# An encoder trunk in fp32r with its normed inputs and weights at their own offsets in longer buffers

## The chip, the cores and the metric

The kernel runs on one core of one Trainium2 chip. The metric is the time on the device in microseconds (us) from the start to the end of one execution, as the median of several. The core has five engines with a queue of instructions each: TensorE (PE in the profile, with its weight loads shown apart as PEld), VectorE (DVE), ScalarE (ACT), GpSimd (POOL) and SyncE (SP), which in this kernel issues most DMA transfers. All work on one on-chip memory of 128 partitions.

## What is computed

A trunk of two layers over 1024 tokens of width 1024, in float32. Each layer norms its input, mixes tokens (layer 0: a gMLP with a spatial gate; layer 1: HGRN2, a gated linear recurrence in chunks of 64), adds the result, norms again and runs a gated FFN with a convolution over three tokens.

```python
for i in range(DEPTH):                       # DEPTH = 2
    mod = (cond @ ada_w[i] + ada_b[i])[:, None, :]
    sh1, sc1, g1, sh2, sc2, g2 = jnp.split(mod, 6, axis=-1)
    h = rms_norm(x, norm_g[i, 0]) * (1.0 + sc1) + sh1
    y = spatial_gating_mixer(h, ...) if i == 0 else hgrn2_mixer(h, ...)
    x = x + g1 * y
    h = rms_norm(x, norm_g[i, 1]) * (1.0 + sc2) + sh2
    x = x + g2 * conv_ffn(h, ...)
return rms_norm(x, final_g)

def conv_ffn(h, w_up, conv_w, conv_b, w_down):
    a = h @ w_up                             # 1024 -> 2 * 2816
    ap = jnp.pad(a, ((0, 0), (CONV_WIDTH - 1, 0), (0, 0)))
    y = conv_b
    for j in range(CONV_WIDTH):              # CONV_WIDTH = 3
        y = y + conv_w[j] * ap[:, j:j + t]
    gate, val = jnp.split(y, 2, axis=-1)
    return (jax.nn.gelu(gate, approximate=False) * val) @ w_down
```

HGRN2's scores inside a chunk are masked to be causal; in the kernel six masks of 64 columns do that, one for each level of a halving of the chunk, times which the scores are multiplied.

## The kernel before

Tokens lie on the free axis: xT holds the residual stream as 8 blocks (kt) of 128 features by 1024 tokens. A product in float32 is made of three in fp32r, the type in which TensorE takes its full rate: each operand is split into a high part and the rest, and `mm3` (line 377) multiplies high by high, low by high and high by low. Nearly all matmuls of the program are those of line 380.

The operands lie in *cells*, buffers of one name each whose type can change over the program. There are 32 n cells of 512 words (name n, the normed input: high and low part, 8 kt, two halves of the tokens), 12 w cells (weights) and 12 h cells of 1024 words. A word is 4 bytes. `Cell.new` (line 75) allocates a cell again under its name. A matmul of the profile that reads "pb<-n,w" has a slice of an n cell as its moving operand and a slice of a w cell as its weights, in "pb<-w,n" the w cell moves, and in "pb<-h,w" an h cell moves. Buffers lie one behind the other in the order in which they are first asked for: prm, xT, n cells, raw (three staging buffers of 1024 words), w cells, h cells, then the arena wk and some small ones. Every length in front of wk is a multiple of 2048 bytes behind prm, so each cell starts at the same place within a 128-byte line.

Weights of the mixers come through `Stream`: SP loads 512 KB into a raw buffer (line 325), ACT copies it into a w cell as the high part (line 335, fp32r), POOL subtracts to get the low part into the next w cell (line 340). In the FFNs (class `Ffn`) the products are made by a scheme of seven block products in place of eight, so sums of weight blocks and of input blocks are formed first; ACT splits them at line 1038 and DVE or POOL subtracts at line 1041. Weights come by DMA straight into w cells (in_up) and into n cells that are no longer read (in_down, line 1052).

What sets the order: in the first stages and in HGRN the code's own order (HGRN as an interleaving of `granules` of one unit with steps of the next). Around the FFNs a planner (`Plan`) is given operations with an engine, a cost, a priority and what they read and write, and deals them out to the engines' queues by its own clock. The last three units of HGRN and FFN 1 are planned together. `plan_out` (lines 520 to 600) plans HGRN's output projection: PE multiplies, and the result is added to xT either by DVE alone (line 544) or by ACT into a temporary (line 554) and POOL from there (line 557). The temporaries are slots that are taken in turn; two slots at first, `sgs.slots[0]` and `spare` (the second half of h cell 5), and a third appended once unit 15 has freed it.

HGRN's arena wk holds two rings of two and one of one buffer each of 512 words and, behind, the six masks, loaded in one DMA of 192 KB (line 1489). `masked` (line 1612) multiplies the scores by a mask at line 1614. The h cells are dealt out as hx (line 1490).

Of the kernel before, what the change touches and what calls it, by code (L numbers as in the profile page):

```python
# [13 lines left out]
P = 128  # L14
D = 1024
KT = D // P
T = 1024
HT = T // 2
# [10 lines left out]
MASKS = ("even", "odd", 2, 4, 8, 16)  # L29

NW = 6
NRAW = 3
WK = 3968
PADW = 2
LAST = 3
NPLAIN = 2

# [20 lines left out]
class Ring:  # L58
    def __init__(self, slots):
        self.slots = slots  # L60
        self.i = 0
# [7 lines left out]
class Cell:  # L69


    def __init__(self, pool, name, n=1024):
        self.pool, self.name, self.n = pool, name, n

    def new(self, dtype):
        return self.pool.tile([P, self.n], dtype, name=self.name, tag=self.name, bufs=1)


class Life:
# [159 lines left out]
def trunk(tc, a, pool, psum, dram):  # L239
    nc = tc.nc  # L240
    V, S, G, PE = nc.vector, nc.scalar, nc.gpsimd, nc.tensor

    prm = pool.tile([P, NPARAM], F32, name="prm")
    xT = pool.tile([P, KT, T], F32, name="xT")
    ncells = {(t, kt, hf): Cell(pool, f"n{t}{kt}{hf}", HT) for t in range(2) for kt in range(KT) for hf in range(2)}
    hlife = {k: Life(c.name, HT, F32R, c, c.new(F32R)) for k, c in ncells.items()}
    rawt = [pool.tile([P, 1024], F32, name=f"raw{i}") for i in range(NRAW)]
    wc, hc = ([Cell(pool, f"{n}{i}") for i in range(12)] for n in "wh")
    wt = [c.new(F32R) for c in wc]
    raws = Ring(list(rawt))  # L250
    whis, wlos = Ring(wt[0::2]), Ring(wt[1::2])
    wk = pool.tile([P, WK], F32, name="wk")
    ones = pool.tile([P, P], F32, name="ones")
# [19 lines left out]
    class Arena:  # L273
        def __init__(self, tile):
            self.t = tile
            self.o = 0
# [420 lines left out]
    spare = [wk[:, 192 + i * 512:704 + i * 512] for i in range(6)]  # L697
# [6 lines left out]
    for d, n in ((0, 2), (2, 2), (4, 2), (6, 1), (7, 1)):  # L704
# [7 lines left out]
           for i in range(2)]  # L712
    cnd = [pl.op("V", 0.6, lambda i=i: V.tensor_tensor(out=condr[:, i * 512:i * 512 + 512],
                                                       in0=condr[:, i * 512:i * 512 + 512], in1=sgm[i], op=ALU.mult),
# [5 lines left out]
    for item in loads.split():  # L720
# [8 lines left out]
        if item == "W":  # L729
            n = len(cvl)  # L730
# [41 lines left out]
    for d in range(KT):  # L772
        t, pr = nb.t.slots[d % 2], d - 0.5
# [8 lines left out]
        for p in range(2):  # L782
# [7 lines left out]
            n = d // 2 * 2 + p + NW  # L790
# [136 lines left out]

    wkl = Life("wk", WK, ap=wk)
    rawl = [Life(f"raw{i}", 1024, ap=t) for i, t in enumerate(rawt)]
    bankl = [Life(f"pb{i}", 512, ap=t) for i, t in enumerate(bank)]  # L930

    def kv(o, n=512):
        return View(wkl, o, n)
# [124 lines left out]
    class Ffn:  # L1058
# [33 lines left out]
        def pads(self):  # L1092
            for i in range(3):
                o = i * (PADW + T)
                self.pl.op("V", 0.1, lambda o=o: V.memset(wk[:, o:o + PADW], 0.0), w=(("wk", o, o + PADW),),
                           pr=self.base - 20)
# [34 lines left out]
        def pair(self, j, fine=False):  # L1131
            pl, l = self.pl, self.l
            g, v, s1 = self.rawset[j % 2]
            if j == NPLAIN:
                s1 = kv(3 * (PADW + T))

# [18 lines left out]

            og, ov = (((2 * j + i) % 3) * (PADW + T) for i in range(2))
            c11, c12, c21, c22 = (kv(o + PADW + x) for o in (og, ov) for x in (0, HT))

# [25 lines left out]
        def plain_pair(self, j, fine):  # L1184
# [4 lines left out]
            def p(i):  # L1189
                return self.base + 7 * j + i  # L1190
# [3 lines left out]
            for c in range(2):  # L1194
                for r, x in enumerate((g, v)):
                    w[r, c] = self.slots.next()
                    p_split(pl, View(x.life, 512 * c, 512), *w[r, c], "G", p(-6 + c))
            os_ = [((2 * j + i) % 3) * (PADW + T) for i in range(2)]
            step = 1 if fine else 4
# [78 lines left out]
        def down(self, after_first, last, ranges=False):  # L1278
# [58 lines left out]
            for i in range(7):  # L1337
# [6 lines left out]
                if i == 5:  # L1344
                    after_first(n_op[0] - 4)
                for m in range(nm if i < 6 else nm - LAST):
                    get(i, m, n_op[0] - 3)
                    for d in range(4):
                        end = m == nm - 1 or (ranges and i == 6 and m == nm - LAST - 1)
                        mm(i, m, d, m == 0, end)  # L1350
                        if end:
                            read(i, d)
            for m in range(nm - LAST, nm):
                get(6, m, n_op[0] - 3)
# [10 lines left out]
            def last_mm(d, o=0, n=HT):  # L1365
                for m in range(nm - LAST, nm):
                    mm(6, m, d, ranges and m == nm - LAST, m == nm - 1, o, n)
                return bv(4 + d, o, n)
# [114 lines left out]
    ha = Arena(wk)  # L1483
# [1 line left out]
    qqs = ha.ring(2, 512)  # L1485
    sts = ha.ring(2, 512)
    tots = ha.ring(1, 512)
    masks = ha.take(len(MASKS) * 64)
    nc.sync.dma_start(masks, a["masks"])
    hx = [c.new(F32) for c in hc[0:10]] + [c.new(F32R) for c in hc[10:12]]  # L1490
    vts = Ring(hx[0:3])
    qxs, q1s, k1s, fs = (Ring([hx[i][:, o:o + n]]) for i, o, n in ((3, 0, 768), (4, 0, 512), (4, 512, 512), (5, 0, 512)))
    spare = hx[5][:, 512:1024]
    mts = Ring([hx[3][:, 768:1024], hx[8][:, 512:768]])
    scs = Ring([hx[8][:, 0:512]])
    sigs, sgs, ots, hph, hpl = (Ring([hx[i][:, 0:512], hx[i][:, 512:1024]]) for i in (6, 7, 9, 10, 11))
# [20 lines left out]
    class Unit:  # L1517
# [92 lines left out]
                PE.matmul(ps[0:m, c, :], self.K[s][:, c * P:c * P + m], q, start=True, stop=True)  # L1610

        def masked(self, out, ps, name, m=P):
            i = MASKS.index(name) * 64
            V.tensor_tensor(out=out[0:m], in0=ps[0:m], in1=masks[0:m, i:i + 64].unsqueeze(1).to_broadcast([m, 4, 64]),  # L1614
                            op=ALU.mult)

        def lv_cut(self, s):
# [212 lines left out]
    nms = [Norm(0), Norm(HT)]  # L1830
    nms[0].acc_slot = (hx[2][:, 0:512], [], [])
    sqs = Slots([rawt[1][:, 0:512], rawt[1][:, 512:1024]])
    tmps = Slots([sgs.slots[0], spare])
    rbv = [rv(2, 0, 512), rv(2, 512, 512)]
    add0, _ = plan_out(pl, [("ho", u14.h)], [u14.act], gate1(1), nms[0], early, sqs, 22, (wait,))
    _, e13 = plan_out(pl, [("ho", u13.h)], [u13.act], gate1(1), nms[1], early, None, 18, (), tmps, "S")
# [9 lines left out]
    for i in old:  # L1846
        for c in hc:
            if c not in (hc[0], hc[2], hc[4]):
                pl._touch(i, (c.name, 0, c.n), False)
        pl._touch(i, ("wk", 0, WK), False)  # L1850
        pl._touch(i, ("raw1", 0, 1024), False)
# [158 lines left out]
```

## Time and profile before

| | |
|---|---|
| median of 2 runs | 2571.52 us (2571.14 to 2571.91) |
| the profiled execution | 2565.72 us |
| its span in the profile | 2563.9 us |
| PE busy | 2471.1 us (96%) |
| PEld busy | 2057.4 us (80%) |
| DVE busy | 2019.3 us (79%) |
| ACT busy | 1068.0 us (42%) |
| POOL busy | 561.2 us (22%) |
| granted TensorE clock, mean | 0.99 |

The profile is of one execution. A row of a group names the source line (L380 is line 380 of the code above), the engine, the operation and its operands by the program's names without buffer numbers, and how often it ran. The views named below are: the windows (busy time of each engine in stretches of the span), the chain of work that ended last (followed back from the last instruction to what released it), the timeline (instructions in order of time, runs of the same kind joined; the bracket gives the engine's idle time before and what ended it), and one tile's or one line's instructions with minimum, median and maximum duration.

### The profile page before, as it was taken

What the parts mean: (1) busy time and instruction counts of PE and PEld (TensorE: products, weight loads), DVE (VectorE), ACT (ScalarE), POOL (GpSimd) and SP (SyncE); (2) the same over time, 40 slices, a digit from 0 to 9 for tenths busy, and PEclk for the clock granted to TensorE, in tenths of its full rate; (3) what the DMA queues carried; (4) which work ended last, traced back from release to release, by engine and by line L of the source; (5) the groups of instructions that cost most, each with busy time, mean ns of one, the idle gap of its engine ahead of it and who ended that gap; (6) DMA issues with size and microseconds to landing.
All of it is one profiled execution on the core that took longest, in us unless ns stands there. A gap on an engine that the chain in (4) does not pass through costs nothing.

```text
span 2563.9 us, 32796 instructions
## 1 busy us (share of the span) xinstructions
PE 2471.1 (96%) x11990; PEld 2057.4 (80%) x11990; DVE 2019.3 (79%) x3237; ACT 1068.0 (42%) x1762; POOL 561.2 (22%) x308
## 2 busy tenths in 40 slices
PE   6999999999999999999999999999979999999997
PEld 4778788787788888888788889888857888888886
DVE  8895766658999898976857676767888998889757
ACT  3322111124555555445533333333445555545444
POOL 3233221111131222013321110211142232220022
PEclk9999999999999999999999999999989999999998
DMA  9795323311233233743111110100101332328333
GB/s 330 260 342 181 115 86 122 121 66 50 70 107 120 99 107 112 279 139 103 53 42 34 34 34 18 50 34 17 42 18 68 109 115 95 119 97 290 98 91 103
DMA packets 122994, 280.03 MB, mean 109 GB/s; under 512 B 12112, under 2 KB 30672, under 8 KB 122832
## 3 DMA queue, kind: packets, MB, share of 16 engines
q1 hardware_dynamic: 105936, 269.54, 31.1%
q10 hardware_dynamic: 16896, 8.39, 1.1%
q8 instruction: 94, 1.54, 0.2%
q14 instruction: 68, 0.56, 0.1%
HBM read 224.93 MB, written 52.95 MB: 108 GB/s over the span
## 4 chain that ended last, share of the span: by engine, by line
PE 75%; DVE 13%; DMA 6%; issue 3%; ACT 2%; POOL 1%; SPq 0%; DVEq 0%; ACTq 0%; POOLq 0%
PE pb L380 69%; PE pb L1610 3%; DMA raw<-in_ada 3%; DVE raw L397 1%; DVE h L397 1%; POOL w L340 1%; DVE raw L1268 1%; DMA raw<-in_wu 1%; DMA raw<-in_wv 1%; DMA n<-in_down 1%; DVE n L1026 1%; PE pb L1662 0%; PE pb L496 0%; DVE wk L464 0%; PE pb L1684 0%
## 5 line engine op out<-in xcount | busy, mean ns | idle before, releaser
L380 PE MATMUL pb<-h,w 128*128 128x512 f32 (+1 forms) x4476 | 1059.6, 391 | 14.2 <-DVE xT L518 9.2
L380 PE MATMUL pb<-n,w 128*128 128x512 f32 x4224 | 1019.8, 395 | 10.5 <-ACT wk L1160 4.6
L380 PEld LDWEIGHTS pb<-h,w 128*128 128x128 f32 x4476 | 830.0, 188 | 192.5 <-DVE xT L518 11.8
L380 PEld LDWEIGHTS pb<-n,w 128*128 128x128 f32 x4224 | 790.9, 189 | 176.8 <-ACT wk L1160 5.9
L340 POOL TENSOR_TENSOR w<-raw,w 128x1024 fp32r<-128x1024 f32 x83 | 208.3, 2520 | 779.6 <-ACT w L335 779.6
L1041 POOL TENSOR_TENSOR w<-w,w 128x512 fp32r<-128x512 f32 x136 | 213.7, 1579 | 701.1 <-ACT w L1038 680.4
L380 PE MATMUL pb<-w,n 128*128 128x512 f32 (+1 forms) x1536 | 279.7, 342 | 9.8 <-ACT n L776 4.9
L1038 ACT ACTIVATE w<-w 128x512 fp32r<-128x512 f32 x330 | 204.1, 627 | 184.6 <-PE pb L380 112.2
L380 PEld LDWEIGHTS pb<-w,n 128*128 128x128 f32 x1536 | 238.8, 192 | 49.1 <-ACT n L776 8.4
L1268 DVE SCALAR_TENSOR_TENSOR raw<-wk,prm,raw 128x1024 f32<-128x1024 f32 x168 | 250.6, 1513 | 18.8 <-ACT raw L1264 16.8
L518 DVE SCALAR_TENSOR_TENSOR xT<-pb,mod,xT 128x512 f32<-128x512 f32 x200 | 145.8, 745 | 39.5 <-PE pb L380 38.6
L335 ACT ACTIVATE w<-raw 128x1024 fp32r<-128x1024 f32 x83 | 87.0, 1057 | 216.0 <-PE pb L380 148.7
L1160 ACT ACTIVATE wk<-pb 128x512 f32<-128x512 f32 x160 | 95.1, 598 | 174.3 <-PE pb L380 161.3
L1041 DVE TENSOR_TENSOR w<-w,w 128x512 fp32r<-128x512 f32 x194 | 141.5, 734 | 27.9 <-ACT w L1038 27.8
L1163 DVE TENSOR_TENSOR wk<-pb,wk 128x512 f32<-128x512 f32 x160 | 109.0, 686 | 49.5 <-PE pb L380 29.8
L1591 ACT ACTIVATE wk<-wk 128x256 f32<-128x256 f32 x192 | 74.2, 415 | 123.3 <-PE pb L1610 94.9
L1264 ACT ACTIVATE raw<-wk,prm 128x1024 f32<-128x1024 f32 x84 | 104.2, 1243 | 42.5 <-DVE wk L1163 34.6
L397 DVE SCALAR_TENSOR_TENSOR raw<-raw,raw 128x1024 f32<-128x1024 f32 x32 | 52.2, 1631 | 77.1 <-DMA raw<-in_ada 77.1
L1038 ACT ACTIVATE w<-n 128x512 fp32r<-128x512 f32 x96 | 60.6, 631 | 116.8 <-PE pb L380 115.3
L1041 DVE TENSOR_TENSOR w<-n,w 128x512 fp32r<-128x512 f32 x96 | 71.8, 750 | 44.0 <-ACT w L1038 43.7
L1614 DVE TENSOR_TENSOR h<-pb,wk 128x256 f32<-128x256 f32 (+1 forms) x96 | 38.8, 418 | 73.4 <-PE pb L1610 48.1
L397 DVE SCALAR_TENSOR_TENSOR h<-h,raw 128x1024 f32<-128x1024 f32 x64 | 91.0, 1435 | 3.2 <-DMA h<-in_ada 3.1
(214 smaller groups left out, 2376.3 us busy)
## 6 DMA issues: line engine op xcount, KB each, us to landing
w<-in_up SPq DMA_DIRECT2D x88, 512.0 KB, 3.7
act<-raw SPq DMA_DIRECT2D x154, 256.0 KB, 2.2
h<-in_ada SPq DMA_DIRECT2D x64, 512.0 KB, 6.3
h<-act SPq DMA_DIRECT2D x124, 256.0 KB, 2.8
raw<-in_ada SPq DMA_DIRECT2D x32, 512.0 KB, 4.1
n<-in_down SPq DMA_DIRECT2D x64, 256.0 KB, 5.4
vd<-h ACTq DMA_DIRECT2D x32, 256.0 KB, 5.4
raw<-in_wu SPq DMA_DIRECT2D x16, 512.0 KB, 4.3
```

The lines of the kernel that those rows point to most:

```text
L335: S.activation(hi, raw, AF.Copy)
L340: G.tensor_tensor(out=lo, in0=raw, in1=hi.bitcast(F32), op=ALU.subtract)
L380: PE.matmul(ps, L[i // 2], R[i % 2], start=first and i == 0 and not more, stop=last and i == 2, skip_group_check=more)
L397: V.scalar_tensor_tensor(out=raw, in0=raw, scalar=1.0, in1=condr, op0=ALU.mult, op1=ALU.mult, accum_out=mod[:, m:m + 1])
L518: V.scalar_tensor_tensor(out=xT[:, d, hs], in0=ps, scalar=gate(d), in1=xT[:, d, hs], op0=ALU.mult, op1=ALU.add)
L1038: pl.op("S", 0.2 + 0.43 * w, lambda: S.activation(hi.r, src.f, AF.Copy), r=(src,), w=(hi,), pr=pr)
L1041: lambda: e.tensor_tensor(out=lo.r, in0=src.f, in1=hi.f, op=ALU.subtract),
L1160: pl.op("S", 0.6, lambda: S.activation(c.f, ps.f, AF.Copy), r=(ps,), w=(c,), pr=p(i) - 10)
L1163: pl.op("V", 0.75, lambda: V.tensor_tensor(out=c.f, in0=ps.f, in1=c.f, op=ALU.add), r=(ps, c), w=(c,), pr=p(i) - 8)
L1264: pl.op("S", 1.15, lambda: S.activation(y.f, wk[:, o + PADW:o + PADW + T], AF.Identity, bias=pc("conv_b", l * NUP + b), scale=cw(2)), r=(c ...
L1268: pl.op("V", 1.17, lambda w=w: V.scalar_tensor_tensor(out=y.f, in0=wk[:, o + w:o + w + T], scalar=cw(w), in1=y.f, op0=ALU.mult, op1=ALU.ad ...
L1610: PE.matmul(ps[0:m, c, :], self.K[s][:, c * P:c * P + m], q, start=True, stop=True)
```

## The change

The n cells become 520 words long and the w cells 1032. Of each the program uses a slice of the old length that begins at a number of words of its own: `N_AT` for the kt of an n cell (0 to 6 words, 0 to 24 bytes), `W_AT` for the number of a w cell. A cell is now 32 bytes longer than before, so cells behind it move by 32 bytes each. The h cells keep their length and have no offset.

The arena wk shrinks from 3968 to 3590 words, since the masks leave it: four of them go into columns 768 to 1024 of h cell 8 and two into columns 512 to 640 of h cell 5, by two DMAs. `spare` had that second half of h cell 5; it goes, so `tmps` begins with one slot. Six lines more in front shift the line numbers: L380 before is L386 after, L1041 is L1047.

```diff
--- before.py
+++ after.py
@@ -30,8 +30,10 @@
 
 NW = 6
 NRAW = 3
-WK = 3968
+WK = 3590
 PADW = 2
+N_AT = (0, 1, 2, 4, 0, 3, 5, 6)
+W_AT = (0, 0, 2, 2, 4, 4, 1, 1, 0, 6, 6, 3)
 LAST = 3
 NPLAIN = 2
 
@@ -69,11 +71,14 @@
 class Cell:
 
 
-    def __init__(self, pool, name, n=1024):
-        self.pool, self.name, self.n = pool, name, n
+    def __init__(self, pool, name, n=1024, off=None):
+        self.pool, self.name, self.n, self.off = pool, name, n, off
 
     def new(self, dtype):
-        return self.pool.tile([P, self.n], dtype, name=self.name, tag=self.name, bufs=1)
+        if self.off is None:
+            return self.pool.tile([P, self.n], dtype, name=self.name, tag=self.name, bufs=1)
+        t = self.pool.tile([P, self.n + 8], dtype, name=self.name, tag=self.name, bufs=1)
+        return t[:, self.off:self.off + self.n]
 
 
 class Life:
@@ -242,10 +247,11 @@
 
     prm = pool.tile([P, NPARAM], F32, name="prm")
     xT = pool.tile([P, KT, T], F32, name="xT")
-    ncells = {(t, kt, hf): Cell(pool, f"n{t}{kt}{hf}", HT) for t in range(2) for kt in range(KT) for hf in range(2)}
+    ncells = {(t, kt, hf): Cell(pool, f"n{t}{kt}{hf}", HT, N_AT[kt]) for t in range(2) for kt in range(KT) for hf in range(2)}
     hlife = {k: Life(c.name, HT, F32R, c, c.new(F32R)) for k, c in ncells.items()}
     rawt = [pool.tile([P, 1024], F32, name=f"raw{i}") for i in range(NRAW)]
-    wc, hc = ([Cell(pool, f"{n}{i}") for i in range(12)] for n in "wh")
+    wc = [Cell(pool, f"w{i}", off=W_AT[i]) for i in range(12)]
+    hc = [Cell(pool, f"h{i}") for i in range(12)]
     wt = [c.new(F32R) for c in wc]
     raws = Ring(list(rawt))
     whis, wlos = Ring(wt[0::2]), Ring(wt[1::2])
@@ -1485,12 +1491,12 @@
     qqs = ha.ring(2, 512)
     sts = ha.ring(2, 512)
     tots = ha.ring(1, 512)
-    masks = ha.take(len(MASKS) * 64)
-    nc.sync.dma_start(masks, a["masks"])
     hx = [c.new(F32) for c in hc[0:10]] + [c.new(F32R) for c in hc[10:12]]
     vts = Ring(hx[0:3])
     qxs, q1s, k1s, fs = (Ring([hx[i][:, o:o + n]]) for i, o, n in ((3, 0, 768), (4, 0, 512), (4, 512, 512), (5, 0, 512)))
-    spare = hx[5][:, 512:1024]
+    masks = [hx[8][:, 768 + i * 64:832 + i * 64] for i in range(4)] + [hx[5][:, 512 + i * 64:576 + i * 64] for i in range(2)]
+    nc.sync.dma_start(hx[8][:, 768:1024], a["masks"][:, 0:256])
+    nc.sync.dma_start(hx[5][:, 512:640], a["masks"][:, 256:384])
     mts = Ring([hx[3][:, 768:1024], hx[8][:, 512:768]])
     scs = Ring([hx[8][:, 0:512]])
     sigs, sgs, ots, hph, hpl = (Ring([hx[i][:, 0:512], hx[i][:, 512:1024]]) for i in (6, 7, 9, 10, 11))
@@ -1610,8 +1616,8 @@
                 PE.matmul(ps[0:m, c, :], self.K[s][:, c * P:c * P + m], q, start=True, stop=True)
 
         def masked(self, out, ps, name, m=P):
-            i = MASKS.index(name) * 64
-            V.tensor_tensor(out=out[0:m], in0=ps[0:m], in1=masks[0:m, i:i + 64].unsqueeze(1).to_broadcast([m, 4, 64]),
+            mask = masks[MASKS.index(name)]
+            V.tensor_tensor(out=out[0:m], in0=ps[0:m], in1=mask[0:m].unsqueeze(1).to_broadcast([m, 4, 64]),
                             op=ALU.mult)
 
         def lv_cut(self, s):
@@ -1830,7 +1836,7 @@
     nms = [Norm(0), Norm(HT)]
     nms[0].acc_slot = (hx[2][:, 0:512], [], [])
     sqs = Slots([rawt[1][:, 0:512], rawt[1][:, 512:1024]])
-    tmps = Slots([sgs.slots[0], spare])
+    tmps = Slots([sgs.slots[0]])
     rbv = [rv(2, 0, 512), rv(2, 512, 512)]
     add0, _ = plan_out(pl, [("ho", u14.h)], [u14.act], gate1(1), nms[0], early, sqs, 22, (wait,))
     _, e13 = plan_out(pl, [("ho", u13.h)], [u13.act], gate1(1), nms[1], early, None, 18, (), tmps, "S")
```

On SP's queue, where HGRN's loads begin (in_masks are the masks, in_hgf and the like its weights), before:

```order
L1052 DMA wk<-act 128x512
L1052 DMA h_6638<-act 128x512 x2
L1489 DMA wk<-in_masks 128x384
L325 DMA raw_97<-in_hgf 128x1024
L325 DMA raw_98<-in_hgg 128x1024
```

and at the same place of SP's queue after (h_8362 is h cell 8, h_8359 h cell 5):

```order
L1058 DMA wk<-act 128x512
L1058 DMA h_6638<-act 128x512 x2
L1498 DMA h_8362<-in_masks 128x256
L1499 DMA h_8359<-in_masks 128x128
L331 DMA raw_97<-in_hgf 128x1024
L331 DMA raw_98<-in_hgg 128x1024
```

One transfer into wk has become two into h cells; they stand at the same place, ahead of the loads of the weights.

On POOL's queue, at the end of HGRN, where unit 15's and 14's output projections are added to xT (L557 before, L563 after) between sums of squares (L581, L587) and the first weights of FFN 1 (L1041, L1047), before:

```order
L1635 TENSOR_TENSOR h_8363<-h_8363 112x16x16
L557 TENSOR_TENSOR xT<-xT,h_8362 128x512
L557 TENSOR_TENSOR xT<-xT,h_8360 128x512
L557 TENSOR_TENSOR xT<-xT,h_8362 128x512
L557 TENSOR_TENSOR xT<-xT,h_8360 128x512 x2
L557 TENSOR_TENSOR xT<-xT,h_8362 128x512
L557 TENSOR_TENSOR xT<-xT,h_8360 128x512
L557 TENSOR_TENSOR xT<-xT,h_8362 128x512
L1041 TENSOR_TENSOR w_12903<-w_12671,w_12903 128x512
L1041 TENSOR_TENSOR w_12907<-w_12684,w_12907 128x512
L581 TENSOR_TENSOR h_8356<-h_8356,raw_98 128x512
L557 TENSOR_TENSOR xT<-xT,h_8358 128x512
```

and there on POOL after, down to the same sum of squares and on:

```order
L1641 TENSOR_TENSOR h_8362<-h_8362 112x16x16
L563 TENSOR_TENSOR xT<-xT,h_8361 128x512 x9
L587 TENSOR_TENSOR h_8355<-h_8355,raw_98 128x512
L1047 TENSOR_TENSOR w_12936<-w_12672,w_12936 128x512
L1047 TENSOR_TENSOR w_12941<-w_12685,w_12941 128x512
L587 TENSOR_TENSOR h_8355<-h_8355,raw_98 128x512
L563 TENSOR_TENSOR xT<-xT,h_8357 128x512
L587 TENSOR_TENSOR h_8355<-h_8355,raw_98 128x512 x2
```

The temporaries h_8362 and h_8360 alternated; one of them is left, nine additions stand in a row, and two of the sums of squares have changed places with the splits of the weights.

On DVE's queue, right behind, where the norm ahead of FFN 1 is applied (L1016 and L1026 before, L1022 and L1032 after, make the n cells) beside additions of the output projection (L544, L550), before:

```order
L1016 SCALAR_TENSOR_TENSOR h_12898<-xT,amul,raw_99 128x512
L1016 SCALAR_TENSOR_TENSOR h_12905<-xT,amul,raw_99 128x512
L1016 SCALAR_TENSOR_TENSOR h_12898<-xT,amul,raw_99 128x512
L544 SCALAR_TENSOR_TENSOR xT<-pb_124,mod,xT 128x512
L544 SCALAR_TENSOR_TENSOR xT<-pb_125,mod,xT 128x512
L544 SCALAR_TENSOR_TENSOR xT<-pb_124,mod,xT 128x512
L544 SCALAR_TENSOR_TENSOR xT<-pb_125,mod,xT 128x512
L1026 SCALAR_TENSOR_TENSOR n_7898<-h_12898,mod,n_7886 128x512
L1026 SCALAR_TENSOR_TENSOR n_7982<-h_12898,mod,n_7973 128x512
L1016 SCALAR_TENSOR_TENSOR h_12905<-xT,amul,raw_99 128x512
L1026 SCALAR_TENSOR_TENSOR n_7935<-h_12905,mod,n_7929 128x512
```

and the same rows of DVE after:

```order
L1022 SCALAR_TENSOR_TENSOR h_12896<-xT,amul,raw_99 128x512
L1022 SCALAR_TENSOR_TENSOR h_12902<-xT,amul,raw_99 128x512
L1022 SCALAR_TENSOR_TENSOR h_12896<-xT,amul,raw_99 128x512
L1032 SCALAR_TENSOR_TENSOR n_7898<-h_12896,mod,n_7886 128x512
L1022 SCALAR_TENSOR_TENSOR h_12902<-xT,amul,raw_99 128x512
L1032 SCALAR_TENSOR_TENSOR n_7982<-h_12896,mod,n_7973 128x512
L1032 SCALAR_TENSOR_TENSOR n_7935<-h_12902,mod,n_7929 128x512
L550 SCALAR_TENSOR_TENSOR xT<-pb_124,mod,xT 128x512
L1032 SCALAR_TENSOR_TENSOR n_8074<-h_12902,mod,n_7995 128x512
L550 SCALAR_TENSOR_TENSOR xT<-pb_125,mod,xT 128x512
L1022 SCALAR_TENSOR_TENSOR h_12943<-xT,amul,raw_99 128x512
```

The first normed inputs are written ahead of the four additions; those stand further back.

## The prediction

> **What bounds the kernel now.** I read the span and the stages first, then the chain that ended last, then the spacing of the matmuls inside an unbroken run, then one line of POOL. Stages of the program, with the busy time (and count) of PE, PEld, DVE, ACT and POOL, the granted clock, and the DMA share and rate:
>
> ```profile
> 600.00:1010.00 410.00, 404.44 (x1775) 332.88 (x1774) 371.74 (x443) 215.30 (x314) 98.44 (x63) 1.00 0.28 98
> 1010.00:1300.00 290.00, 286.32 (x1329) 238.05 (x1328) 222.88 (x330) 141.61 (x236) 58.76 (x33) 0.99 0.43 136
> 1330.00:1700.00 370.00, 366.13 (x2256) 320.46 (x2257) 266.34 (x612) 132.85 (x285) 62.94 (x26) 1.00 0.11 38
> 1900.00:2330.00 430.00, 422.43 (x1845) 346.89 (x1845) 380.67 (x453) 223.70 (x325) 101.50 (x63) 0.99 0.31 106
> sum 2564.00, PE 2471.11 PEld 2057.44 DVE 2019.27 ACT 1068.01 POOL 561.15; mean PE 190.09 PEld 158.26 DVE 155.33 ACT 82.15 POOL 43.17
> ```
>
> PE is busy for 98% or more of each of these stages, at the full clock. DVE is second (372 of 410 us in the first FFN's up-projection), POOL is far off with 561 of 2564 us. The page's chain says the same, and the two longest unbroken pieces of the chain in order of time show what it is made of:
>
> ```profile
> PE 75%; DVE 13%; DMA 6%; issue 3%; ACT 2%; POOL 1%; SPq 0%; DVEq 0%; ACTq 0%; POOLq 0%
> PE pb L380 69%; PE pb L1610 3%; DMA raw<-in_ada 3%; DVE raw L397 1%; DVE h L397 1%; POOL w L340 1%; DVE raw L1268 1%; DMA raw<-in_wu 1%; DMA raw<-in_wv 1%; DMA n<-in_down 1%; DVE n L1026 1%; PE pb L1662 0%; PE pb L496 0%; DVE wk L464 0%; PE pb L1684 0%
> 731.72 472.34 PE pb L380 x2079
> 1973.57 342.85 PE pb L380 x1503
> ```
>
> 472.34 us / 2079 is 227.2 ns for a matmul, 342.85 / 1503 is 228.1. So the time is a count of matmuls times their spacing, and the question is whether the new addresses change the spacing. Here it is cleaner, in two runs without a gap, and with the durations of single matmuls and weight loads (min/median/max, ns):
>
> ```profile
> 1280.94 23.20 PE L380 MATMUL pb<-w,n 128*128 128x256 f32 x192
> 2312.98 5.60 PE L380 MATMUL pb<-n,w 128*128 128x512 f32 x24
> L380 PE MATMUL pb<-w,n x1536: 277/376/796, 21.4 to 1751.8; 128*128 128x512 f32 x96, 128*128 128x256 f32 x96
> L380 PE MATMUL pb<-n,w x4224: 387/389/799, 219.9 to 2329.1; 128*128 128x512 f32 x192
> L380 PEld LDWEIGHTS pb<-n,w x4224: 186/188/337, 219.7 to 2328.9; 128*128 128x128 f32 x192
> ```
>
> The end of a row is the end of its last matmul, so the spacing of 512 columns is (5.60 - 0.39) / 23 = 226.5 ns, that of 256 columns (23.20 - 0.28) / 191 = 120.0 ns. The difference, 106.5 ns, is the price of 256 columns; what is left, 120.0 - 106.5 = 13.5 ns, comes with each matmul whatever its width. A weight load takes 188 ns and runs beside the matmul before it, so it doesn't set 226.5. All 10236 matmuls of L380 (9396 of 512 columns, 840 of 256) carry these 13.5 ns: 138 us in all. In the build of before, every n, w and h cell starts at the same place within a 128-byte line (96 bytes in), so the trace holds no such matmul at another place. That is the resource it does not show.
>
> **The change, part by part.** *Matmul operands.* No matmul is added or removed. In the build of after, the moving operand of 4248 of the 10236 no longer starts at a multiple of 32 bytes (n cells with offset 1 to 6 words, and the w cells where they are the moving operand), the weights of 7492 don't, and the two operands of 7946 differ in their place within 32 bytes; before, all agreed. The h cells, which have no offset, are pushed by the longer cells ahead of them to multiples of 128 bytes, so that 5108 moving operands start there (4476 of h). Bounds for one matmul: the 13.5 ns vanish (-13.5), or come twice (+13.5). Which value, between ends so far apart? The nearest row is one where the two operands stand apart already or the weight is absent from the path:
>
> ```profile
> 174.66 1.88 PE L645 MATMUL pb<-wk,ones 128*128 128x512 f32 x4
> L645 PE MATMUL pb<-wk,ones x4: 590/592/592, 174.7 to 175.9; 128*128 128x512 f32 x4
> ```
>
> These four have the same 512 columns at half rate: (1.88 - 0.59) / 3 = 430 ns, against 2 x (226.5 - 13.5) = 426 for the columns alone. So the fixed part isn't a price of each matmul whatever it reads; but it isn't shown to hang on an address either, since these differ in rate too. The matmuls with the same shape and every combination of cells before (n, h or w moving) have one duration, 387 to 389 ns, whether the next load is beside them or not, so I see no strife between the two reads that a shifted start could ease. I take 0 for the spacing and keep -13.5 and +13.5 for the rivals.
>
> The Trainium skill, "TensorE: Matmul & The Clock Gate", step-by-step part, says that TensorE has two independent SBUF read ports, one for the streaming operand and one for the weights, and that loading the next weights takes no read bandwidth from the running matmul; by that rule the relation of the two addresses is worth nothing, and the sum would be the one I forecast. That it is not the last word shows in the 13.5 ns, which the page's own gap does not have (below).
>
> *POOL.* The lower halves of the weights are made at L1041 (w<-w,w) and L340 (w<-raw,w). Here the trace does show a place effect:
>
> ```profile
> L1041 POOL TENSOR_TENSOR h<-h,h x32: 1287/1288/6162, 1133.7 to 2531.4; 128x512 fp32r<-128x512 f32 x32
> L1041 POOL TENSOR_TENSOR h<-wk,h x8: 1092/1098/2627, 1128.8 to 2513.4; 128x512 fp32r<-128x512 f32 x8
> L1041 POOL TENSOR_TENSOR w<-w,w x136: 1276/1378/3496, 564.3 to 2313.7; 128x512 fp32r<-128x512 f32 x136
> L340 POOL TENSOR_TENSOR w<-raw,w x83: 2367/2400/3397, 30.9 to 1772.7; 128x1024 fp32r<-128x1024 f32 x83
> ```
>
> The same operation takes 1.288 us where both inputs start alike and 1.098 where the first is the slice of wk, which lies 24 bytes into a 32-byte line: 0.19 us less. After, 128 of the 136 w<-w,w have inputs at unlike places: 128 x 0.19 = 24 us of POOL's 561. L1041 on POOL is in no share of the chain that the page lists; the cover is PE (404 of 410 us in the up-projection). L340 is 1%, that is some 26 us or 11 instructions; if a 1024-column one gains twice 0.19, the path gains 11 x 0.38 = 4 us, if nothing, 0. I take -3. DVE's own operations of this line keep 0.68 us with either source, so DVE gains nothing itself; it waits less beside a shorter POOL:
>
> ```profile
> L1041 DVE TENSOR_TENSOR h<-h,h x110: 671/683/2492, 637.2 to 2533.2; 128x512 fp32r<-128x512 f32 x110
> L1041 DVE TENSOR_TENSOR h<-wk,h x22: 678/684/687, 1042.5 to 2530.9; 128x512 fp32r<-128x512 f32 x22
> L1041 DVE TENSOR_TENSOR w<-w,w x194: 673/682/1787, 656.1 to 2518.3; 128x512 fp32r<-128x512 f32 x194
> ...
> L1041 DVE TENSOR_TENSOR w<-w,w 128x512 fp32r<-128x512 f32 x194 | 141.5, 734 | 27.9 <-ACT w L1038 27.8
> ```
>
> DVE's share of the chain is 13%; of some 10 us that its w<-w,w spend over their median (194 x (734 - 682) ns, the page's mean against the median) a tenth lies there: -1, bounds 0 and -3.
>
> *Masks.* One load of 192 KB becomes two, the second into h cell 5, which PE still reads:
>
> ```profile
> 1242.30 0.33 SPq L1489 DMA_DIRECT2D wk<-in_masks  x1
> 1260.98 0.33 SPq L325 DMA_DIRECT2D raw<-in_hgf  x1
> 1238.80 19.88 PE L380 MATMUL pb<-h,w 128*128 128x512 f32 x87
> 1264.52 1.06 ACT L335 ACTIVATE w<-raw 128x1024 fp32r<-128x1024 f32 x1 [4.33 <-DMA raw<-in_hgf]
> L1614 DVE TENSOR_TENSOR h<-pb,wk x96: 407/416/427, 1305.0 to 1851.6; 128x256 f32<-128x256 f32 x48, 124x256 f32<-124x256 f32 x16, 120x256 f32<-120x256 f32 x16, 112x256 f32<-112x256 f32 x16
> ```
>
> SP's queue is in order: behind the wait stand the loads of HGRN's weights, and ACT's queue stands behind the first of them. PE's last read of the h cells ends at 1258.68, SP issues the next load only at 1260.98: the wait ends 2.3 us early, and one more issue costs 0.33. First use of the masks is at 1305. So 0, at worst the 4.33 us of idle again, +5.
>
> *Slots in HGRN's end.* With one slot in place of two, ACT's L554 and POOL's L557 alternate on one buffer:
>
> ```profile
> 1857.72 1.29 POOL L557 TENSOR_TENSOR xT<-xT,h 128x512 f32<-128x512 f32 x1 [3.85 <-ACT h L554]
> 1868.61 2.48 POOL L557 TENSOR_TENSOR xT<-xT,h 128x512 f32<-128x512 f32 x2 [0.70 <-ACT h L554]
> L554 ACT ACTIVATE h<-pb,mod x10: 670/687/690, 1857.0 to 1884.8; 128x512 f32<-128x512 f32 x10
> 1872.35 0.99 PE L1710 MATMUL pb<-prm,h 128*128 128x128 f32 x4 [4.61 <-DVE h L1702]
> 1895.35 4.86 PE L380 MATMUL pb<-n,w 128*128 128x512 f32 x11 [0.38 <-DVE n L1026]
> ```
>
> Eight additions took 1857.72 to 1871.09, 13.4 us; in turn with 0.69 of ACT they take 8 x (1.29 + 0.69) = 15.8. PE waits at this place for DVE's norm, not for POOL. DVE's and PE's orders behind it are dealt anew: in after the first n is normed and multiplied ahead of the remaining output projection, the last n stands at nearly the same row (2256 against 2254), and up to that one PE waits in both. -3 to +3 us, I take +1.
>
> *Transfers into cells at odd starts* (n<-in_down, w<-in_up) have no row of their own. The chain shows these:
>
> ```profile
> 2316.42 5.47 DMA n<-in_down
> 2321.90 5.57 DMA n<-in_down
> 2327.49 4.39 DMA n<-in_down
> ```
>
> They are 15.4 us of FFN 1; 10% on them, an estimate, is +1.5; I take 0.
>
> **Sum.** The profiled execution took 2565.72 (span 2563.9 and 1.8 around it); 2565.72 - 3 - 1 + 1 = 2562.7. It lies 5.8 below the median of the two runs shown, 2571.52, so against that median 2568.5. Own range: from 4 + 3 + 3 us less to 5 + 3 + 1.5 more, 2561 to 2581. Some 2% (51 us) is what a measurement of this kernel surely tells from no change.
>
> **The rivals.** *A, faster: the 13.5 ns belong to where the moving operand starts.* All start 96 bytes into a 128-byte line before, and so read one line more than a start at 0 would: 17 lines in place of 16, at 13.3 ns each 226.7 and for 256 columns 9 x 13.3 = 120.0, which are the two spacings measured. That speaks for it. Against it: the half-rate row above shows 4 ns over, not 13 or 27. After, 5108 start at 0 and lose it: 5108 x 13.5 = 69 us. The chain holds 69% of 2564 = 1769 us of L380, whose spacing times count is 9396 x 226.5 + 840 x 120.0 = 2229 us, so some 79% lies on it: -55, 2514 us.
>
> *B, faster: two operands at the same place in a 32-byte line cost it*, as POOL's row suggests of another engine. 7946 pairs are apart afterwards: 107 us, 79% of it 85: 2484 us. In the up-projection PE would go from 404 to about 386 (1775 x 13.5 ns x 0.78 less), still above DVE's 372. Against it: the same duration with and without a load beside. The Trainium skill, "TensorE: Matmul & The Clock Gate", back-to-back issue gap, gives columns / 2.4 + 2.5 ns, 215.8 for 512 columns; the trace's 226.5 is 10.7 above it. By that rule the surplus is no fixed price of a matmul, and taken off the 7946, 79% on the chain, it would give -67 us; no run here shows such a spacing.
>
> *S, slower: a moving operand that starts off a 32-byte line costs one line more.* 4248 x 13.5 = 57 us, all on PE, where nothing covers it: 2568.5 + 57 = 2626 us. It decides from (51.4 + 3) / 4248 = 12.8 ns a matmul on. The weights off a line don't count: 188 + 13 ns still fit within 226.5. For it: the line arithmetic of A reads the same way for shorter lines. Against it: on DVE, sources with unlike starts take the same time (0.683 and 0.684 above).
>
> *That the change does little of what it says* as far as TensorE goes is the forecast itself: 4476 of the moving operands, all of h, have no offset and still start at a multiple of 32 bytes.
>
> **How the numbers follow.** As forecast, 0.53; A 0.18; B 0.12; S 0.17. Faster by over 2%: 0.30, within: 0.53, slower: 0.17. The predicted time is the likeliest case's, 2568.5, its own range 2561 to 2581. The range on record leaves out S (0.17) and reaches down to B: 2480 to 2581.
>
> **What would show it.** The unbroken run of 24 matmuls of n,w at 5.60 us and that of 192 of w,n at 23.20 us again: my forecast. Down to 5.29 (23 x 13.5 ns less) in runs with h moving, with most of n unchanged: A; in most runs of either: B; up to 5.91 in n,w alone: S. POOL's w<-w,w at about 1.10 us instead of 1.29, with POOL some 24 us less busy and the chain's L340 share a little smaller, shows that step right; 1.29 shows it wrong. The load of in_hgf issued after 1261.5 shows the masks' wait on the path. A spacing that changes by more than 3 ns in either sense makes the forecast wrong.

## The result and the profile after

The changed kernel takes 2606.65 us (2606.28 to 2607.02, 2 runs) against 2571.52 us; the ratio is 1.0137 with a 95% interval of 1.0093 to 1.018. It is slower by about 35 us, or 1.4%, above both ranges of the forecast, which end at 2581 us.

The page of the changed kernel, busy times and chain (compare 2471.1 us of PE before, and a chain with 75% of PE and 69% of L380):

```profile
span 2604.5 us, 32798 instructions
...
PE 2523.6 (97%) x11990; PEld 2063.5 (79%) x11990; DVE 1996.4 (77%) x3237; ACT 1070.0 (41%) x1762; POOL 520.4 (20%) x308
...
PE 84%; DVE 8%; DMA 4%; issue 2%; ACT 1%; POOL 1%; SPq 0%; DVEq 0%; ACTq 0%; POOLq 0%
PE pb L386 77%; PE pb L1616 3%; DMA raw<-in_ada 3%; DVE raw L403 1%; DVE h L403 1%; POOL w L346 1%; PE pb L1668 1%; PE pb L502 0%; PE pb L1690 0%; PE pb L1692 0%; DVE h L696 0%; PE pb L492 0%; DVE h L897 0%; PE pb L1716 0%; DVE amul L415 0%
```

The span grew by 40.6 us. PE is busy 52.5 us longer with the same 11990 instructions, and idle 11.9 us less (2604.5 - 2523.6 = 80.9 against 2563.9 - 2471.1 = 92.8). POOL shrank by 41 us and DVE by 23. So nothing new is waited for: the matmuls themselves take longer, and the rest of the kernel gives a little back.

The chain of the changed kernel in order of time, its two longest unbroken pieces:

```profile
630.73 415.58 PE pb L386 x1779
2000.04 531.61 PE pb L386 x2271
```

415.58 / 1779 is 233.6 ns for a matmul, 531.61 / 2271 is 234.1, where it was 227.2 and 228.1. The timeline of the changed kernel in the first up-projection, and its run of 192 matmuls of 256 columns:

```profile
916.52 2.95 PE L386 MATMUL pb<-h,w 128*128 128x512 f32 x12
919.31 2.97 PE L386 MATMUL pb<-n,w 128*128 128x512 f32 x12
922.11 2.97 PE L386 MATMUL pb<-h,w 128*128 128x512 f32 x12
924.92 5.79 PE L386 MATMUL pb<-n,w 128*128 128x512 f32 x24
...
1306.04 22.84 PE L386 MATMUL pb<-w,n 128*128 128x256 f32 x192
```

Twelve matmuls of h,w take 919.31 - 916.52 = 2.79 us to the start of the next run, 232.5 ns each, though h cells have no offset; 24 of n,w take 5.79 where they took 5.60. The run of 256 columns went the other way, from 23.20 to 22.84. Taken over all matmuls of L380 before and L386 after that have another of the same line behind them (gaps over 260 ns left out), the mean spacing is:

| ns from start to start | h,w, 512 columns | its 10th and 90th percentile | n,w, 512 | w,n, 256 |
|---|---|---|---|---|
| before | 227.1 | 226, 227 | 227.3 | 121.2 |
| after | 232.9 | 229, 237 | 233.6 | 120.1 |

Some 6.0 ns for 9396 matmuls are 56 us, -1.1 for 840 are -1; PE's busy time, in which the matmuls' ends are modelled, shows 52.5 of these 55. Less the 11.9 us of idle time given back, that is the 40.6 us of the span.

### The profile page after: what moved, and what is told of

Its sections match the earlier page's. It is cut to its first block, busy times and chain, and to the rows that moved or that the text cites. A ratio compares the mean times of both kernels' runs of the same rounds, so it can differ in the third digit from the quotient of the medians.

```text
span 2604.5 us, 32798 instructions
## 1 busy us (share of the span) xinstructions
PE 2523.6 (97%) x11990; PEld 2063.5 (79%) x11990; DVE 1996.4 (77%) x3237; ACT 1070.0 (41%) x1762; POOL 520.4 (20%) x308
## 4 chain that ended last, share of the span: by engine, by line
PE 84%; DVE 8%; DMA 4%; issue 2%; ACT 1%; POOL 1%; SPq 0%; DVEq 0%; ACTq 0%; POOLq 0%
PE pb L386 77%; PE pb L1616 3%; DMA raw<-in_ada 3%; DVE raw L403 1%; DVE h L403 1%; POOL w L346 1%; PE pb L1668 1%; PE pb L502 0%; PE pb L1690 0%; PE pb L1692 0%; DVE h L696 0%; PE pb L492 0%; DVE h L897 0%; PE pb L1716 0%; DVE amul L415 0%
## 5 line engine op out<-in xcount | busy, mean ns | idle before, releaser
L386 PE MATMUL pb<-h,w 128*128 128x512 f32 (+1 forms) x4476 | 1084.4, 396 | 11.2 <-DVE xT L524 8.6
L386 PE MATMUL pb<-n,w 128*128 128x512 f32 x4224 | 1044.5, 400 | 10.8 <-DVE n L1032 5.5
L386 PEld LDWEIGHTS pb<-h,w 128*128 128x128 f32 x4476 | 832.0, 189 | 211.5 <-DVE xT L524 11.2
L386 PEld LDWEIGHTS pb<-n,w 128*128 128x128 f32 x4224 | 794.1, 190 | 198.0 <-DVE n L1032 6.6
L346 POOL TENSOR_TENSOR w<-raw,w 128x1024 fp32r<-128x1024 f32 x83 | 192.6, 2330 | 804.8 <-ACT w L341 804.8
L1047 POOL TENSOR_TENSOR w<-w,w 128x512 fp32r<-128x512 f32 x136 | 192.9, 1426 | 737.7 <-ACT w L1044 444.3
L386 PE MATMUL pb<-w,n 128*128 128x512 f32 (+1 forms) x1536 | 282.0, 344 | 7.1 <-ACT n L782 3.2
L386 PEld LDWEIGHTS pb<-w,n 128*128 128x128 f32 x1536 | 239.0, 191 | 48.4 <-ACT n L782 5.5
L1047 DVE TENSOR_TENSOR w<-w,w 128x512 fp32r<-128x512 f32 x194 | 137.9, 715 | 36.3 <-ACT w L1044 36.3
L1047 DVE TENSOR_TENSOR w<-n,w 128x512 fp32r<-128x512 f32 x96 | 70.3, 735 | 49.3 <-ACT w L1044 48.6
L1620 DVE TENSOR_TENSOR h<-pb,h 128x256 f32<-128x256 f32 (+1 forms) x96 | 38.9, 419 | 75.7 <-PE pb L1616 49.6
```

Source lines behind the costliest of these rows:

```text
L346: G.tensor_tensor(out=lo, in0=raw, in1=hi.bitcast(F32), op=ALU.subtract)
L386: PE.matmul(ps, L[i // 2], R[i % 2], start=first and i == 0 and not more, stop=last and i == 2, skip_group_check=more)
L1047: lambda: e.tensor_tensor(out=lo.r, in0=src.f, in1=hi.f, op=ALU.subtract),
```

## The experiments

Eleven runs. m0_masks, z_zero, n_only and w_only are edits of the changed kernel; m32_masks and those whose name begins with k_ start from m0_masks. In the k_ runs the code has one line more, so that L387 there is L386 of the changed kernel. "Distance" is the start of the moving operand less that of the weights, modulo 512 bytes at first, modulo 256 later. Starts are the addresses that the buffers have in each program. By these the arena wk lies between the w cells and the h cells, and not behind the h cells as the description of the kernel ahead has it; so the arena's length moves the h cells.

**The rest of the change, without offsets.** The edit against the changed kernel:

```diff
-WK = 3590
+WK = 3712
-    ncells = {...: Cell(pool, f"n{t}{kt}{hf}", HT, N_AT[kt]) ...}
+    ncells = {...: Cell(pool, f"n{t}{kt}{hf}", HT) ...}
-    wc = [Cell(pool, f"w{i}", off=W_AT[i]) for i in range(12)]
+    wc = [Cell(pool, f"w{i}") for i in range(12)]
```

> The masks in h cells and one slot less, but no longer buffers and no offsets; the arena is 3712 words, so that all operand cells start at the same place within 512 bytes as in the kernel before. Theory R (relation): a full-rate 512-column matmul keeps 226.7 ns as long as its moving operand starts at the same place within 512 bytes as the weights that are loaded beside it, and takes some 6 ns more where it does not; here all are alike, so spacing 226.7 and the time of before within 5 us. Theory O (off the line): only starts that are no multiple of 32 bytes cost; also the time of before. Theory M (masks, slots and order): the loss comes from the rest of the change; some 2605 us.

Measured: 2570.52 us (2567.91 to 2573.67, 10 runs), ratio to before 0.9997 (0.9987 to 1.0006). Spacing 227.1 (h,w), 227.3 (n,w), 121.2 (w,n), as before. The masks, the missing slot and the new order in HGRN's end cost nothing that can be measured; theory M falls. PE is idle 89.8 us here (92.8 before).

**The h cells alone moved by 32 bytes.** The same with one number changed:

```diff
-WK = 3712
+WK = 3590
```

> As the run before it, but the arena is 3590 words as in the change, which moves the h cells, and them alone, by 32 bytes against all others. R: the 4369 matmuls with h moving take 6 ns more, those with n moving 226.7; +26 us less what waits take in, 2585 to 2600 us. O: no start is off 32 bytes, so as the run before it. A line of 128 bytes for the moving operand (rival A of the prediction): h is faster by 13 ns.

Measured: 2595.71 us, ratio 1.0102 (1.0085 to 1.0119). The timeline of this kernel in the first up-projection:

```profile
915.04 2.97 PE L386 MATMUL pb<-h,w 128*128 128x512 f32 x12
917.84 2.92 PE L386 MATMUL pb<-n,w 128*128 128x512 f32 x12
920.60 2.97 PE L386 MATMUL pb<-h,w 128*128 128x512 f32 x12
```

h,w takes 2.80 us to the next run (233.3 ns each), n,w beside it 2.76, and over the kernel the means are 233.4 and 228.3, w,n 121.1. Every start here is a multiple of 32 bytes, and h starts at a multiple of 512. So theory O falls (no start off a line is needed for the loss), and with it rival A of the prediction: h at the start of a 128-byte line is slower, not faster. Of the three families of operands one number has moved the h cells alone, and it has made about three quarters of the change's loss (1.0102 against 1.0137). The profile has 4476 matmuls with h moving, not the 4369 of the expectation.

**The offsets at zero, buffers long.**

```diff
-N_AT = (0, 1, 2, 4, 0, 3, 5, 6)
-W_AT = (0, 0, 2, 2, 4, 4, 1, 1, 0, 6, 6, 3)
+N_AT = (0,) * 8
+W_AT = (0,) * 12
```

> The change with all offsets zero: the buffers are as long as in the change, so the cells step by 32 bytes more each, but every one starts at a multiple of 32 bytes. R: nearly all pairs start apart, so the spacing is that of the change (some 233 ns) and the time 2600 to 2610 us. O: spacing 226.7 and 2560 to 2575 us. POOL: the splits gain nothing if their gain hangs on the place within 32 bytes (1.29 us again).

Measured: 2608.21 us, ratio 1.0146 (1.0131 to 1.0161); spacing 232.7, 232.3 and 119.7. The whole loss without any offset: it is the eight words by which the buffers are longer that do it, since each cell then begins 32 bytes further than the one ahead. POOL's splits stayed at their old times; the offsets within 32 bytes are what POOL answers to. From its page:

```profile
span 2604.8 us, 32798 instructions
...
PE 2520.3 (97%) x11990; PEld 2061.6 (79%) x11990; DVE 2021.3 (78%) x3237; ACT 1069.1 (41%) x1762; POOL 559.1 (21%) x308
```

PE is idle 2604.8 - 2520.3 = 84.5 us here, 8.3 less than before, with POOL as long as before. So by these profiles, one of each kernel, most of the 11.9 us of idle time that the changed kernel gave back does not come from POOL.

**One family at a time.** The same two lines as in m0_masks, each alone, with the arena at 3590 words.

> Only the n cells longer and offset; w as before, h 32 bytes aside. R: nearly all pairs apart, 2595 to 2610 us, spacing some 233 in n,w and h,w. O: only n cells off 32 bytes (3168 of 4224) cost 6 ns or more, h,w stays at 226.7: some 2585 us.

> Only the w cells longer and offset, n as before, h 96 bytes aside. R: nearly all pairs apart, spacing some 233 ns as in the change, and POOL's splits of weights shorter as in the change (some 40 us of POOL): 2595 to 2607 us. If the offsets within 32 bytes cost spacing by themselves, n,w here, with n on a 32-byte line and w off it, is 1 to 2 ns above the 232.3 of z_zero.

n_only: 2610.19 us, ratio 1.0155 (1.014 to 1.017); 233.2 (h,w), 233.4 (n,w), 119.6. w_only: 2600.27 us, ratio 1.0109 (1.0092 to 1.0126); 232.8, 232.5, 120.1; POOL 522.9 us. n_only ends 0.2 us above its expected range. Either family alone brings the full spacing, since either puts over 90% of the pairs apart. With the n cells off a 32-byte line n,w stands 1.1 ns above z_zero's, with w off it 0.2: what the offsets add by themselves is some fifth of the 6 ns at most here, though the distances are not z_zero's either. The span of w_only is 9.8 us below that of n_only: PE is busy 5.7 us less (2518.6 against 2524.3) and idle 4.1 us less, beside a POOL that is 35 us shorter.

**Place or relation.** m32_masks moved h to another place and to another distance from w at once. A gap ahead of the w cells moves w and h together:

```diff
     rawt = [pool.tile([P, 1024], F32, name=f"raw{i}") for i in range(NRAW)]
+    pool.tile([P, 8], F32, name="padw")
```

> As m0_masks, with 32 bytes of gap ahead of the w cells: w and h start at multiples of 512 bytes, n 32 bytes short of one. Theory R (relation of the moving operand to the weights that are loaded beside it): h,w are alike, 226.7 ns, n,w apart, 233; some 2590 us. Theory P (the place itself: a start at a multiple of 512 costs, as h had it in m32_masks): h,w 233 and n,w 226.7. By the time alone the two can't be told apart, by the spacing they can.

Measured: 2590.48 us, ratio 1.0077 (1.0053 to 1.0102). The timeline of this kernel:

```profile
916.32 2.91 PE L387 MATMUL pb<-h,w 128*128 128x512 f32 x12
919.06 2.96 PE L387 MATMUL pb<-n,w 128*128 128x512 f32 x12
921.86 2.91 PE L387 MATMUL pb<-h,w 128*128 128x512 f32 x12
```

h,w is back at 2.74 us for twelve (228.3 ns; mean over the kernel 227.7), n,w now takes 2.80 (233.3; mean 233.4). h is at the place that cost it 6 ns in m32_masks, and pays nothing as w is there too; n is where it always was, and pays. It is the relation, and theory P falls.

**Other distances.** Gaps of 16 and 32 words ahead of w, and the arena at 3648 and 3728 words:

> As m0_masks, with w 64 bytes behind n and h 256 bytes before w (within 512). R with any distance alike: n,w and h,w at 233 ns, some 2605 us. If the price follows the distance, the two differ from 233 and from each other; if the period is 256 bytes, h,w is back at 226.7.

> As k_scan with other distances: w starts 128 bytes behind n, h 64 bytes behind w (both modulo 256). k_scan had 226.7 ns for a moving start 256 bytes from the weights, so the period is at most 256. R with a period of 128: n,w back at 226.7, h,w some 229 to 233; with a period of 256: n,w some 233 too.

k_scan: 2590.64 us, k_scan2: 2596.35 us, one run each. Means by distance, with m32_masks and k_place (w is w,n: the w cell moves):

| distance, bytes modulo 256 | 512 columns, ns | 256 columns, ns |
|---|---|---|
| 0 (h in k_scan, 256 bytes away) | 227.7 | 121.0 |
| 32 (h in m32_masks; w in k_place) | 233.4; 233.3 | 117.9; 118.1 |
| 64 (h in k_scan2; w in k_scan) | 229.4; 229.2 | 115.3; 119.1 |
| 128 (n and w in k_scan2) | 232.6 and 232.4 | 120.3 |
| -64 (n in k_scan) | 233.3 | |
| -32 (n in k_place) | 233.4 | |

A distance of 256 bytes is as good as none, 128 is not; a period of 256 fits, as far as this one distance shows. The price is not the same at all distances (64 costs 2, 32 and -64 cost 6), so the expectation that every distance costs alike was wrong. The one in k_scan2 that 64 bytes would cost 2 to 6 ns held. With 256 columns the spacing falls, by 1 to 6 ns; at 64 it has two values, so there the distance is not all that counts.

**What the fixed part is.** Two kernels in which some matmuls use 64 of the 128 weight columns, and so leave out part of their product:

```diff
         for i in part:
-            PE.matmul(ps, L[i // 2], R[i % 2], ...)
+            m = 64 if i == 1 else P
+            PE.matmul(ps[0:m], L[i // 2][:, 0:m], R[i % 2], ...)
```

> As m0_masks, but the second of each three products loads and uses only the first 64 of 128 weight columns (half of that product is left out). Theory L (the 13.3 ns over the columns are stolen from the moving operand by the reads of the load beside it): a matmul with a 64-column load beside it (the first of three) falls to 220.0 ns, the other two stay at 226.7. Theory F (13.3 ns are a fixed price of a matmul): all three stay at 226.7.

and with

```diff
+            m = P if (first and i == 0) or (last and i == 2) else 64
```

> As m0_masks, but of the 24 matmuls of each group of sums all but the first and the last load and use only 64 of 128 weight columns (half of the output is left out). k_load64b, with every third load so, had lost the even spacing, 224 to 236 ns; here 22 loads in a row are equal again. Theory L (reads of the load beside it hold the moving operand): even spacing returns, at about half the surplus, 220.0 ns. Theory F (fixed price of 32 cycles): 226.7. Theory T (an even spacing needs full loads): 224 to 236 as in k_load64b.

Measured: 2587.12 and 2581.63 us, one run each; means over 512 columns (h,w) 229.8 and 229.6. The timeline of the second, and its run of 192:

```profile
917.42 2.92 PE L387 MATMUL pb<-h,w 128*128 128x512 f32 x12
...
1296.34 22.08 PE L387 MATMUL pb<-w,n 128*128 128x256 f32 x192
```

At 512 columns the spacing went up and is no longer even in either kernel: it swings between 224 and 236 ns (in stretches 235, 230, 224 in turn), as theory T had it, and neither L nor F did. At 256 columns it is even and fell from 120.0 to (22.08 - 0.28) / 191 = 114.1, near the half surplus of theory L (106.5 + 6.7 = 113.2). That is no proof of L: in k_scan2 half of the h,w of 256 columns have 113 ns (the median) with full loads, at a distance of 64 bytes. What is shown is that the 13.5 ns are no fixed price: fewer weight columns change the spacing of matmuls whose moving operand and whose starts are the same. The edit shortens the load and narrows the matmul itself at once, so which of the two does it isn't shown, and what sets the size at 512 columns stays open.

**A version that keeps the relation and takes POOL's gain.** Against m0_masks the three raw buffers start 8, 40 and 72 bytes further, all 8 bytes aside modulo 32; a gap puts w and all behind it back at their places modulo 512:

```diff
-    rawt = [pool.tile([P, 1024], F32, name=f"raw{i}") for i in range(NRAW)]
+    rawt = [pool.tile([P, 1032], F32, name=f"raw{i}")[:, 2:1026] for i in range(NRAW)]
+    pool.tile([P, 104], F32, name="padw")
```

> As m0_masks, but the raw buffers start 8 bytes aside of all other cells; they are no operand of TensorE. Matmul spacing 226.7 as before. POOL's 1024-column splits from raw, whose first input then differs by 8 bytes from the second: 2.00 us in place of 2.40 for 83 of them, 33 us of POOL; on the path the share of this line was 1%, so 0 to 8 us faster than m0_masks.

Measured: 2558.7 us (2557.34 to 2559.86), ratio to before 0.995 (0.9935 to 0.9964). It is faster than both kernels. From its page:

```profile
span 2557.4 us, 32798 instructions
...
PE 2475.0 (97%) x11990; PEld 2060.1 (81%) x11990; DVE 1995.2 (78%) x3237; ACT 1068.5 (42%) x1762; POOL 524.3 (21%) x308
```

and the line of POOL's split from raw, with least, median and greatest duration in ns:

```profile
L347 POOL TENSOR_TENSOR w<-raw,w x83: 1994/2001/2985, 31.0 to 1765.0; 128x1024 fp32r<-128x1024 f32 x83
```

The split takes 2.00 us in place of 2.40, POOL is 31 us shorter than in m0_masks (555.7), DVE 21 (2016.4), and PE as busy as there (2476.5), with the spacing of before (227.1, 227.3, 121.2). PE's idle time fell from 2566.3 - 2476.5 = 89.8 us to 2557.4 - 2475.0 = 82.4. The medians are 11.8 us apart where 0 to 8 were expected, the profiled spans 8.9. Ten small matmuls do read raw, against the expectation's words, but none of L387.

## Why the prediction was wrong

- **The spacing.** The step that failed is "I take 0 for the spacing". Its reason was that all combinations of n, h and w had one duration, with or without a load beside, "so I see no strife between the two reads that a shifted start could ease". But all of those combinations had the distance 0, as the prediction itself said; a trace of one distance can't price another, and I asked only whether a shift could ease a strife, not whether it could bring one about. The row that I called the nearest (wk,ones) was no exception: its two starts lie a multiple of 256 bytes apart too, and it runs at half rate. The measured term is +6.0 ns for a matmul of 512 columns and -1.1 for one of 256.
- **Its bounds** of -13.5 and +13.5 ns held it. The range did not: it reached down to rival B (0.12) and stopped at +10 us on the other side, and S, at 2626 us, was left out although I gave it the larger chance (0.17). Had S been in the range, the measured time would have lain in it by luck, as the next point shows.
- **Rival S** had the sign. It had the wrong mechanism: it charged the 4248 matmuls whose moving operand starts off a 32-byte line, at 13.5 ns. What is charged are nearly all of the 9396 with 512 columns, h,w among them, at 6.0. z_zero has no such start and loses as much.
- **Rival A** (start within a 128-byte line) and **rival B** (the same place costs) both fall: in m32_masks h gained nothing at a line's start, and in k_place equal places are the cheap ones. The line arithmetic of A matched both spacings, 226.7 and 120.0, and was still a coincidence.
- **The rule of the Trainium skill** that was weighed, two independent read ports for the moving operand and the weights ("TensorE: Matmul & The Clock Gate", step-by-step part), would have the relation of the two addresses worth nothing. The runs here differ from it: h at one and the same place modulo 512 takes 227.7 ns with w at a distance of 0 (k_place) and 233.4 with w 32 bytes apart (m32_masks). The same page's gap of columns / 2.4 + 2.5 ns, which it calls the isolated one, was not reached either; the lowest mean of any run at 512 columns is 227.1.
- **POOL** was right in sign and nearly in size: w<-w,w 213.7 to 192.9 us, 21 less where I had 24. But the condition is finer. In the changed kernel:

```profile
L1047 POOL TENSOR_TENSOR w<-w,w x136: 1093/1302/2749, 570.3 to 2350.1; 128x512 fp32r<-128x512 f32 x136
...
L346 POOL TENSOR_TENSOR w<-raw,w x83: 1995/2390/3164, 30.7 to 1798.5; 128x1024 fp32r<-128x1024 f32 x83
```

  Sorted by the difference of the two inputs' starts, modulo 16 bytes: 8 or 12 (first input less second) gives the short time (67 of w<-w,w, the least 1.093 us; 46 of the 93 of L346, 83 of them w<-raw,w, the least 1.995), 0 or 4 the long one (69, the least 1.288; 47, the least 2.372). About half of the instructions gained, where I had counted 128 of 136 (by the addresses 134 stand apart modulo 32), and those of L346 gained too.
- **What POOL is worth on the path.** I had -3 us from L340's 1% of the chain and -1 from DVE. For the changed kernel that fits about: PE is idle 80.9 us there and 84.5 in z_zero, where POOL kept its old times (one profile each). Where all of L346 gains it is worth more: k_raw8 is 11.8 us below m0_masks. The chain does not show why: the share of this line is 1% in both, and how much of the gain goes through DVE, 21 us shorter in the same run, was not tried by itself.
- **The masks** cost nothing, as forecast. SP's queue in the changed kernel, and the last matmuls of h,w ahead of it:

```profile
1272.50 0.33 SPq L1498 DMA_DIRECT2D h<-in_masks  x1
1283.72 0.33 SPq L1499 DMA_DIRECT2D h<-in_masks  x1
1285.96 0.33 SPq L331 DMA_DIRECT2D raw<-in_hgf  x1
...
1261.81 21.88 PE L386 MATMUL pb<-h,w 128*128 128x512 f32 x93
```

  The second load waits for the matmuls' end at 1283.69 and goes out at 1283.72; the next goes out 2.27 us after that end, before it was 2.30. The wait named in the prediction is there and ends early. (The mark of 1261.5 us that the prediction set for it is of no use, as everything comes some 25 us later here.)
- **The slots** cost PE nothing: POOL's additions now come one by one, each behind ACT,

```profile
1884.03 1.29 POOL L563 TENSOR_TENSOR xT<-xT,h 128x512 f32<-128x512 f32 x1 [4.65 <-ACT h L560]
1886.12 1.28 POOL L563 TENSOR_TENSOR xT<-xT,h 128x512 f32<-128x512 f32 x1 [0.81 <-ACT h L560]
...
1904.34 1.72 POOL L563 TENSOR_TENSOR xT<-xT,h 128x512 f32<-128x512 f32 x1 [2.62 <-ACT h L560]
```

  2.09 us apart where nothing else is waited for (I had 1.29 + 0.69). But the eight took until 1906.06, 22.0 us in place of the 15.8 worked out, since ACT kept POOL waiting longer at some. The 8801st and the 9201st matmul of the program, which enclose this stretch, start 26.1 and 26.2 us later than before, counted from the span's start: 0.1 was lost between them. In m0_masks, with the spacing of before, nothing was lost (1.9 and 1.7 us later). I had +1.
- **The transfers** into cells at odd starts land as before (n<-in_down 5.4 us, w<-in_up 3.7 in both pages).

## What to carry to other kernels

Buffers that lie one behind the other and whose lengths are all multiples of 256 bytes start their operands alike without anyone having decided it. Before a buffer of such a kernel is made a few words longer, look at what the new steps do to the distance between each matmul's moving operand and its weights, and keep it a multiple of 256 bytes. Move the staging buffers, and leave the operands of the many matmuls alone: 8 bytes on the staging buffers brought 12 us here, 32 bytes more from operand to operand cost 37 (z_zero). And a trace in which nothing varies doesn't say what a duration depends on: a term for which it has one value only needs a run of its own before it is put at 0.

## What the runs showed of the hardware

- The spacing of full-rate fp32r matmuls depends on the distance between the start of the moving operand and of the weights, 256 bytes counting as none: at 512 columns 227.1 to 228.3 ns at a distance of 0, 229 at 64, 232 to 233 at 32, 128, -32 and -64. At 256 columns it is the other way, 121 at 0 and 115 to 120 elsewhere. In these runs the matmul's own weights and those loaded beside it start alike. In z_zero and w_only they often don't, and what counts is still not settled: at 512 columns 235 matmuls of z_zero at 0 to their own weights alone have 232.3 ns, 222 at 0 to those of the next matmul alone 231.9; in w_only it is 235.0 (226) and 232.0 (235).
- Where distances change from one matmul to the next, the distance of the single matmul says little. In z_zero n,w at distance 0 has 230.9 ns and not 227, against 232.5 for the rest; in w_only it has 233.3, against 232.4. Why a matmul at distance 0 loses its spacing among others was not tried by itself.
- GpSimd's subtraction of two SBUF inputs takes 0.19 us less for 512 columns and 0.39 for 1024 when the inputs' starts differ by 8 or 12 bytes modulo 16. A few did not follow: the one w<-wk,w of 1024 columns took 2.385 us in the kernel before at a difference of 8. DVE's subtraction of the same line showed no such dependence (medians of 0.683 us for h<-h,h and 0.684 for h<-wk,h before), but DVE ran 21 us shorter in all beside the shorter POOL of k_raw8.
